# Two-block transformer layer on one core: sliding-window attention units of eight heads instead of four, one small sum on GpSimd, other pacing of stream transposes and first norm

## The chip, the core and the metric

One NeuronCore of one Trainium2 chip runs the whole program. The engines are TensorE (PE in the profile; PEld is its weight load), VectorE (DVE), ScalarE (ACT), GpSimd (POOL) and SyncE (SP, which issues the DMAs here). The metric is the device time of one execution in microseconds, median of three runs.

## The reference

Input is `x` of 512 tokens by 1024 features. Two blocks follow each other. Everything is float32.

The first block normalises `x`, projects it eight ways, does a four-head differential attention and a short gated convolution, projects back, adds, and gates in a per-layer embedding. The second block has a gated MLP (layer A) and then layer B, sliding-window attention with sinks and ALiBi, which the change touches:

```python
q, z = jnp.split(h @ w_in, 2, axis=-1)          # b_w_in_2: 1024 -> 2 x 1024
q = q * (HEAD_DIM ** -0.5)                       # 16 heads of 64, 4 key/value heads
...
logits = jnp.einsum('btkgd,bskd->bkgts', qb, kb).astype(jnp.float32) + alibi
logits = jnp.where(valid, logits, -jnp.inf)      # blocks of 128 queries, 256 keys (first: 128)
m = jnp.maximum(jnp.max(logits, axis=-1), sink)
p = jnp.exp(logits - m[..., None])
denom = jnp.sum(p, axis=-1) + jnp.exp(sink - m)
o = jnp.einsum('bkgts,bskd->btkgd', p.astype(vb.dtype), vb).astype(jnp.float32)
o = o / denom.transpose(0, 3, 1, 2)[..., None]
...
y = out * jax.nn.silu(z)
return y @ w_out                                 # b_w_out_2: 1024 -> 1024
```

The result is normalised, scaled and added to the residual stream `h`.

## The kernel before, in words

**Numbers as pairs.** A float32 operand of a large matmul is split into a high and a low part (`...h`, `...l`): ScalarE copies the high part, VectorE subtracts it from the source for the low part (`gsplit`, `wsplit`). Each product is then three matmuls (`mm3`: high-high, high-low, low-high). Weights come by DMA (`raw`), are split into `whi` and `wlo` in halves of 512 columns, and are used once.

**Who sets the order.** The program is unrolled in Python, and a small planner (`Flow`) decides in which order instructions are written. The main stream is the large matmuls. Everything else is generators; each `yield` says what the next piece waits for: tiles, a condition, or a number of nanoseconds of the planner's PE time. After every three matmuls `F.tick()` lets those continue whose time has come, and what they issue is written at that place. So the planner's costs and the PACE numbers fix, at build time, the order on every engine; on the chip each engine works strictly in that order. When the main stream needs an operand that no generator has delivered yet, `F.until` lets waiting generators go on first.

**The start.** The first projection (`w_in`) runs while `first_stat` forms the sum of squares of `x`: eight squares on ScalarE, seven sums `sq` on VectorE. `norm(st, D, "n1")` then writes the column sums (`st`, four small matmuls), the power on GpSimd and the broadcast (`bc`), and the evictions of the first projection wait for the result.

**Layer B.** The main stream is 16 column blocks of `b_w_in` (24 matmuls each): blocks 0 to 7 give the queries (`QB`), blocks 8 to 15 the gate (`bz`, then `bzt`, `bzs`, in `SZB`). Then comes `b_w_out`, in two halves of two token blocks; in each half the features `k` = 0 to 7 follow each other, so that the attention output `YB[k, t]` is needed for `k` = 4 only after 24 matmuls. `swa_master` spawns an attention unit every PACE_B: for a head group `pr` (0, 1), a block `b` of 128 queries (0 to 3) and a half `s`, four heads. A unit writes, with waits between: eight score matmuls (`bsc`), four additions with running maximum on VectorE (`be`, `bmx`), `bneg` and a sum `bdn` with the sink (VectorE, four elements wide), four exponentials with row sums (ScalarE), the denominator and its reciprocal `brd` (VectorE), the normalisation of two heads on GpSimd and two on ScalarE, per key block four transposes (`btr`) and their split (`bph`, `bpl`), the product with the values (`bpv`), and the joining into `y` (`pc` on ScalarE, `y` on VectorE). The second of the two units of a (`pr`, `b`) then multiplies `y` by the gate in four pieces and splits it into `ybh` and `ybl`, which `b_w_out` reads.

**The end.** `h_tokens` transposes the residual stream back to tokens (`ht`, eight groups of four transposes, PACE_H apart), and `ev_last` scales, adds it and stores.

Of the kernel before, what the change touches and what calls it, by code (L numbers as in the profile page):

```python
# [43 lines left out]
KLATE = 3  # L44
BANKS = 7

PACE_A, PACE_B, PACE_LN, PACE_H = 4500, 3500, 8000, 7000
WARM = 10


# [103 lines left out]
def block(ctx: ExitStack, tc: tile.TileContext, xT, pT, w_in, w_out, w_ple, w_gate, a_w_in, a_w_out,  # L154
# [27 lines left out]
    def pst(name):  # L182
        live[0] += name in COUNTED
        return psum.tile([P, T], F32, tag="ps", name=nm(name))

    def pfree(n=1):
        live[0] -= n

    def banks(n):
        return lambda: live[0] + n <= BANKS  # L190

    def sm(name, n):
        return small.tile([P, n], F32, tag=f"s{n}", name=nm(name), bufs=40 if n == NT else 6)

    def size(a):
        return math.prod(a.shape[1:])
# [4 lines left out]
    def act(o, a, func, bias=0.0, scale=1.0, accum_out=None, after=0.0):  # L201
        nc.scalar.activation(o, a, func, bias=bias, scale=scale, accum_out=accum_out)  # L202
        ex = is_ap(bias, scale, accum_out)
        F.op("act", 80 + 0.84 * size(o) + 93 * len(ex), [o] + is_ap(accum_out), [a] + is_ap(bias, scale), after)

    def stt(o, a, sc, b, op0, op1):
        nc.vector.scalar_tensor_tensor(o, a, sc, b, op0, op1)
        F.op("dve", 70 + 1.04 * size(o) + 65 * len(is_ap(sc)), [o], [a, b] + is_ap(sc))

    def tt(o, a, b, op, after=0.0):  # L210
        nc.vector.tensor_tensor(o, a, b, op)  # L211
        F.op("dve", 70 + 1.04 * size(o), [o], [a, b], after)
# [40 lines left out]
    def transpose(o, a):  # L253
        nc.tensor.transpose(o, a, ident)
        F.op("pe", 114, [o], [a])
# [121 lines left out]
    def gsplit(src, d, key, name, gain=None, dst=None):  # L377
        hi, lo = dst or rt2(name)
        if gain is None:
            act(hi, src, AF.Copy)  # L380
        else:
            act(hi, src, AF.Copy, scale=gain)
        yield [hi]
        if gain is None:
            tt(lo, src, hi.bitcast(F32), ALU.subtract)
        else:
            stt(lo, src, gain, hi.bitcast(F32), ALU.mult, ALU.subtract)
        if d is not None:
            d[key] = (hi, lo)
# [62 lines left out]
    def norm(stat, d, name, n=1024, eps=EPS, copy=True, half=None):  # L452
        key = name if half is None else (name, half)
        yield lambda: all(stat.n[h] == stat.total for h in ((0, 1) if half is None else (half,)))
        yield stat.acc if half is None else [stat.acc[half]]
        r = cols(stat.acc, n, eps, half)
        d[name + "c" if half is None else (name + "c", half)] = r
        yield [r]
        if name in WIDE:
            os = []  # L460
            yield from bcast_wide(r, os)
            o = os[0]
        else:
# [179 lines left out]
    def scores(o, q, k):  # L643
        mm(o, q, k[0], True, False)
        mm(o, q, k[1], False, True)
# [468 lines left out]
    sinkp = const.tile([P, 16], F32, name="sinkp")  # L1114
    tt(sinkp, row[:, R_SINK:R_SINK + 16], cst[:, H_ISL:H_ISL + 16], ALU.mult)

    PO = {}

    def swa_unit(pr, b, s):
        nb = 1 if b == 0 else 2  # L1120
        kw = nb * P
        ksl = slice((b + 1) * P - kw, (b + 1) * P)
        bq = slice(b * P, (b + 1) * P)
        h0 = 8 * pr + 4 * s
        mx = sm("bmx", 4)
        sums = sm("bsum", 4)
        yield banks(2)
        os = [pst("bsc"), pst("bsc")]
        oo = [os[i // 2][:, (i % 2) * 256:(i % 2) * 256 + kw] for i in range(4)]
        for i in range(4):  # L1130
            scores(oo[i], QB[4 * pr + i][s][:, bq], [a[:, ksl] for a in KS[pr][s]])
        yield os
        es = [rt("be"), rt("be")]
        ev = [es[i // 2][:, (i % 2) * 256:(i % 2) * 256 + kw] for i in range(4)]
        for i in range(4):
            addmax(ev[i], oo[i], tbB[:, 256 - kw:], sinkp[:, h0 + i:h0 + i + 1], mx[:, i:i + 1])
        pfree(2)
        neg = sm("bneg", 4)
        tt(neg, mx, cst[:, H_NSL + h0:H_NSL + h0 + 4], ALU.mult)
        for i in range(4):  # L1140
            act(ev[i], ev[i], AF.Exp, bias=neg[:, i:i + 1], scale=SLOPE_B[h0 + i], accum_out=sums[:, i:i + 1])
        dn = sm("bdn", 4)
        tt(dn, neg, row[:, R_SINK + h0:R_SINK + h0 + 4], ALU.add)
        act(dn, dn, AF.Exp)
        yield [dn]
        tt(dn, dn, sums, ALU.add)
        rd = sm("brd", 4)
        recip(rd, dn)
        for i in range(4):
            if i < 2:  # L1150
                nc.gpsimd.tensor_scalar(ev[i], ev[i], rd[:, i:i + 1], None, ALU.mult)
                F.op("pool", 450 + 2.37 * size(ev[i]), [ev[i]], [ev[i], rd])
        yield [rd]
        for i in range(2, 4):
            act(ev[i], ev[i], AF.Copy, scale=rd[:, i:i + 1])
        yield es
        hd = 2 * pr + s
        pts = []
        for kb in range(nb):
            yield banks(1)  # L1160
            o = pst("btr")
            for i in range(4):
                transpose(o[:, i * P:(i + 1) * P], ev[i][:, kb * P:(kb + 1) * P])
            pts.append({})
            yield from gsplit(o, pts[-1], 0, "bp")
            pfree()
        yield [a for p in pts for a in p[0]]
        yield lambda: all(b - nb + 1 + kb in VZ for kb in range(nb))
        yield banks(1)
        o = pst("bpv")  # L1170
        for kb in range(nb):
            v = VZ[b - nb + 1 + kb][:, hd * P:(hd + 1) * P]
            for j in range(2):
                mm(o, v, pts[kb][0][j], kb == j == 0, kb == nb - 1 and j == 1)

        own, other = (LO, HI) if s == 0 else (HI, LO)
        yield [o]
        c = rt("pc")
        act(c[own], o[other], AF.Copy)
        yield [c]  # L1180
        if (pr, b) not in PO:
            PO[pr, b] = [rt("y4"), 0]
        y = PO[pr, b][0]
        tt(y[own], o[own], c[own], ALU.add)
        pfree()
        PO[pr, b][1] += 1
        if PO[pr, b][1] == 2:
            yield lambda: all(4 * pr + i in SZB for i in range(4))
            yield [y, SZB[4 * pr + 3]]
            for i in range(4):  # L1190
                yi = y[:, i * P:(i + 1) * P]
                stt(yi, yi, 0.5, SZB[4 * pr + i][:, bq], ALU.mult, ALU.mult)
            got = {}
            yield from gsplit(y, got, 0, "yb")
            for i in range(4):
                YB[4 * pr + i, b] = [a[:, i * P:(i + 1) * P] for a in got[0]]

    def swa_master():
        for pr, b in ORDER_B:
            yield lambda: pr in KS and all(4 * pr + i in QB for i in range(4))  # L1200
            yield [q for i in range(4) for q in QB[4 * pr + i]] + [k for ks in KS[pr] for k in ks]
            for s in range(2):
                F.spawn(swa_unit(pr, b, s))
                yield PACE_B

    HT = {}

# [166 lines left out]
```

## Time and profile before

| | us |
|---|---|
| median of 3 runs (lowest, highest) | 894.44 (894.09, 894.47) |
| profiled execution, its own time | 895.67 |
| its span, first to last instruction | 893.9 |
| PE busy in it | 881.7 |
| DVE busy | 640.9 |
| ACT busy | 444.2 |
| POOL busy | 72.4 |
| granted clock of PE, mean (share of 2.4 GHz) | 0.999 |

The span is that of the profiled execution, which took 1.23 us longer than the median. A matmul of 512 columns is shown with some 0.39 us, but the next starts about 0.23 us after it: they overlap, and the distance of two starts is the price in a row of them. DVE and ACT instructions overlap by some 0.08 us in the same way.

### The profile page before, as it was taken

The numbers are of one execution on the slowest core, as the hardware profiler recorded it, in microseconds if no ns is written. First come the engines' busy times: TensorE is split into PE (matmuls) and PEld (weight loads), VectorE is DVE, ScalarE is ACT, GpSimd is POOL, SyncE is SP. The second block draws the span as 40 slices with busy tenths as digits, with TensorE's granted clock in tenths as the row PEclk, the third lists the DMA queues.
The fourth block names the chain that finished last, engine by engine and source line by source line (L and its number), as shares of the span: only waits on it lengthen the run. The fifth ranks groups of instructions, "written<-read, shape, count | busy, mean of one in ns | idle before, by whom it ended". The sixth has DMA issues, their size and how long they took to land.

```text
span 893.9 us, 12071 instructions
## 1 busy us (share of the span) xinstructions
PE 881.7 (99%) x4348; PEld 743.6 (83%) x4348; DVE 640.9 (72%) x1380; ACT 444.2 (50%) x954; POOL 72.4 (8%) x77
## 2 busy tenths in 40 slices
PE   8999999999999999999999999999999999999997
PEld 7888888888888888888888888888899988888786
DVE  6899989653558883338897766683347876999974
ACT  7456554322556544335443333322444646998764
POOL 0100113000000001001000000000000001433000
PEclk9999999999999999999999999999999999999999
DMA  7231221225423243232232222314232258211362
GB/s 262 95 119 48 68 99 48 95 94 189 142 71 117 72 134 107 98 105 79 74 112 86 83 95 95 95 51 138 94 121 69 71 145 216 65 48 48 118 198 108
DMA packets 30444, 93.21 MB, mean 104 GB/s; under 512 B 3888, under 2 KB 4272, under 8 KB 30384
## 3 DMA queue, kind: packets, MB, share of 16 engines
q1 hardware_dynamic: 30384, 92.44, 31.8%
q8 instruction: 34, 0.56, 0.3%
q14 instruction: 26, 0.21, 0.1%
HBM read 85.60 MB, written 2.10 MB: 98 GB/s over the span
## 4 chain that ended last, share of the span: by engine, by line
PE 89%; DVE 6%; DMA 1%; ACT 1%; issue 1%; SPq 1%; DVEq 0%; ACTq 0%
PE a_w_in L244 29%; PE w_in L244 18%; PE a_w_out L244 10%; PE b_w_in L244 6%; PE w_gate L244 5%; PE w_out L244 5%; PE b_w_out L244 5%; PE kv L244 3%; PE sp L244 2%; PE e L244 1%; PE sc L244 1%; DVE be L227 1%; PE bsc L244 1%; DVE bpl L211 1%; PE pv L244 1%
## 5 line engine op out<-in xcount | busy, mean ns | idle before, releaser
L211 DVE TENSOR_TENSOR wlo<-raw,whi 128x512 fp32r<-128x512 f32 x280 | 190.5, 708 | 97.4 <-ACT whi L202 96.9
L202 ACT ACTIVATE whi<-raw 128x512 fp32r<-128x512 f32 x280 | 165.5, 623 | 128.5 <-PE a_w_in L244 39.4
L244 PE MATMUL a_w_in<-h2h,whi 128*128 128x512 f32 x256 | 99.8, 390 | 0.0
L244 PE MATMUL a_w_in<-h2l,whi 128*128 128x512 f32 x256 | 99.7, 390 | 0.0
L244 PE MATMUL a_w_in<-h2h,wlo 128*128 128x512 f32 x256 | 99.6, 389 | 0.0
L244 PE MATMUL w_in<-h1h,whi 128*128 128x512 f32 x224 | 88.5, 397 | 0.9 <-ACT h1h L202 0.9
L244 PE MATMUL w_in<-h1h,wlo 128*128 128x512 f32 x224 | 87.0, 391 | 0.0
L244 PE MATMUL w_in<-h1l,whi 128*128 128x512 f32 x224 | 86.9, 390 | 0.0
L215 POOL TENSOR_TENSOR rstd<-var,mhalf 128x4 f32<-128x4 f32 (+2 forms) x15 | 14.1, 939 | 593.5 <-DVE var L222 536.7
L244 PEld LDWEIGHTS a_w_in<-h2h,wlo 128*128 128x128 f32 x256 | 48.1, 188 | 9.9
L244 PEld LDWEIGHTS a_w_in<-h2h,whi 128*128 128x128 f32 x256 | 48.1, 188 | 9.7
L244 PEld LDWEIGHTS a_w_in<-h2l,whi 128*128 128x128 f32 x256 | 48.1, 188 | 9.6
L211 DVE TENSOR_TENSOR sq<-sq,sq 128x512 f32<-128x512 f32 (+1 forms) x44 | 29.3, 666 | 36.3 <-ACT sq L202 34.4
L244 PE MATMUL b_w_in<-hbh,whi 128*128 128x512 f32 x128 | 52.0, 406 | 0.0
L244 PE MATMUL b_w_in<-hbh,wlo 128*128 128x512 f32 x128 | 50.1, 391 | 0.0
L244 PE MATMUL b_w_in<-hbl,whi 128*128 128x512 f32 x128 | 50.1, 391 | 0.0
L244 PE MATMUL a_w_in<-whi,h2h 128*128 128x512 f32 x128 | 50.0, 391 | 0.0
L244 PE MATMUL a_w_in<-whi,h2l 128*128 128x512 f32 x128 | 49.8, 389 | 0.0
L244 PE MATMUL a_w_in<-wlo,h2h 128*128 128x512 f32 x128 | 49.8, 389 | 0.0
L244 PEld LDWEIGHTS w_in<-h1h,whi 128*128 128x128 f32 x224 | 42.0, 188 | 9.2 <-ACT h1h L202 1.1
L244 PEld LDWEIGHTS w_in<-h1h,wlo 128*128 128x128 f32 x224 | 42.0, 188 | 9.0
L244 PEld LDWEIGHTS w_in<-h1l,whi 128*128 128x128 f32 x224 | 42.1, 188 | 8.1
(269 smaller groups left out, 2029.8 us busy)
## 6 DMA issues: line engine op xcount, KB each, us to landing
raw<-in_a_w_in SPq DMA_DIRECT2D x48, 512.0 KB, 3.2
raw<-in_w_in SPq DMA_DIRECT2D x29, 512.0 KB, 3.2
raw<-in_a_w_out SPq DMA_DIRECT2D x16, 512.0 KB, 3.2
raw<-in_b_w_in SPq DMA_DIRECT2D x16, 512.0 KB, 3.5
raw<-in_b_w_out SPq DMA_DIRECT2D x16, 512.0 KB, 3.7
raw<-in_w_out SPq DMA_DIRECT2D x8, 512.0 KB, 3.3
raw<-in_w_gate SPq DMA_DIRECT2D x8, 512.0 KB, 3.3
x<-in_xT SPq DMA_DIRECT2D x8, 256.0 KB, 5.7
```

What stands on the lines that cost most here:

```text
L202: nc.scalar.activation(o, a, func, bias=bias, scale=scale, accum_out=accum_out)
L211: nc.vector.tensor_tensor(o, a, b, op)
L215: nc.gpsimd.tensor_tensor(o, a, b, op)
L227: nc.vector.tensor_tensor_reduce(o, a, b, 1.0, s0, ALU.add, ALU.max, mx)
L244: nc.tensor.matmul(o, a, b, start=start, stop=stop)
```

## The change

One unit now takes the eight heads of a (`pr`, `b`). It makes two rounds of scores and additions (`s` = 0, 1), then one `bneg`, one sum with the sink (eight wide, now on GpSimd), eight exponentials, one denominator and one reciprocal, four normalisations on GpSimd and four on ScalarE, and then per `s` transposes, product and joining; the gate follows. Units start 7000 ns apart (a pair of the old ones took 2 x 3500), the `ht` groups 4000 instead of 7000 ns apart, and `norm` of `n1` waits 1500 ns of the planner's time before its `st` matmuls are written. The buffers of the small tiles follow the new widths.

```diff
-PACE_A, PACE_B, PACE_LN, PACE_H = 4500, 3500, 8000, 7000
+PACE_A, PACE_B, PACE_LN, PACE_H = 4500, 7000, 8000, 4000
...
+        if name == "n1":
+            yield 1500
         r = cols(stat.acc, n, eps, half)
...
-    def swa_unit(pr, b, s):
+    def swa_unit(pr, b):
...
+        mx = sm("bmx", 8)
+        sums = sm("bsum", 8)
+        es = []
+        for s in range(2):
+            yield banks(2)
+            os = [pst("bsc"), pst("bsc")]
...
+            for i in range(4):
+                h = 4 * s + i
+                addmax(es[h // 2][:, (i % 2) * 256:(i % 2) * 256 + kw], oo[i], tbB[:, 256 - kw:],
+                       sinkp[:, h0 + h:h0 + h + 1], mx[:, h:h + 1])
+            pfree(2)
...
+        neg = sm("bneg", 8)
+        tt(neg, mx, cst[:, H_NSL + h0:H_NSL + h0 + 8], ALU.mult)
+        dn = sm("bdn", 8)
+        nc.gpsimd.tensor_tensor(dn, neg, row[:, R_SINK + h0:R_SINK + h0 + 8], ALU.add)
+        F.op("pool", 300, [dn], [neg])
+        for h in range(8):
+            act(ev[h], ev[h], AF.Exp, bias=neg[:, h:h + 1], scale=SLOPE_B[h0 + h], accum_out=sums[:, h:h + 1])
...
+        for h in range(8):
+            if h % 4 < 2:
+                nc.gpsimd.tensor_scalar(ev[h], ev[h], rd[:, h:h + 1], None, ALU.mult)
...
-            for s in range(2):
-                F.spawn(swa_unit(pr, b, s))
-                yield PACE_B
+            F.spawn(swa_unit(pr, b))
+            yield PACE_B
```

Three places of the order. The first is PE at the start of the program, where the four `st` matmuls (column sums of the squares, `sq`) stand among the matmuls of the first projection:

```order
 L244 MATMUL w_in_192<-h1l_176,whi_166 128x512
 L244 MATMUL w_in_192<-h1h_175,wlo_167 128x512
-L244 MATMUL st_299<-ones,sq_209 128x1 x4
 L244 MATMUL w_in_193<-h1h_175,whi_166 128x512
 L244 MATMUL w_in_193<-h1l_176,whi_166 128x512
...
 L244 MATMUL w_in_191<-h1l_181,whi_237 128x512
 L244 MATMUL w_in_191<-h1h_180,wlo_238 128x512
+L244 MATMUL st_314<-ones,sq_209 128x1 x4
```

The sums moved behind nine more matmuls, of which the last is the first to read `wlo_238`.

The second place is VectorE in the order before, from the eviction of the last `b_w_in` block (`bz`, it needs that block's last matmul) to the low part of the output of (`pr`, `b`) = (1, 1), `ybl_8193`; (1, 0) is `ybl_8166`:

```order
L211 TENSOR_TENSOR bz_8070<-b_w_in_7963,n6rb_6574 128x512
L211 TENSOR_TENSOR bpl_8010<-btr_8004,bph_8009 128x512
L211 TENSOR_TENSOR bpl_8029<-btr_8023,bph_8028 128x512
...
L207 SCALAR_TENSOR_TENSOR y_1706_8110<-y_1706_8110,bzs_8122 128x128
L211 TENSOR_TENSOR ybl_8166<-y_1654_7918,ybh_8165 128x512
L211 TENSOR_TENSOR y_1729_8207<-bpv_8149,pc_8172 64x512
L211 TENSOR_TENSOR wlo_8155<-raw_8035,whi_8154 128x512
L211 TENSOR_TENSOR ybl_8193<-y_1706_8110,ybh_8192 128x512
```

These are 28 instructions, both ends counted: 20 of 512 columns and 8 pieces of the gate of 128.

The same stretch of VectorE in the changed kernel, again from the eviction of the last `b_w_in` block to the output of (1, 1), here `ybl_8150` (`y_1544`); (1, 0) is `ybl_8011`:

```order
L211 TENSOR_TENSOR bz_7934<-b_w_in_7840,n6rb_6574 128x512
L211 TENSOR_TENSOR wlo_7763<-raw_7574,whi_7762 128x512
L211 TENSOR_TENSOR wlo_7842<-raw_7691,whi_7841 128x512
L211 TENSOR_TENSOR ybl_7885<-y_1430_7080,ybh_7884 128x512
L211 TENSOR_TENSOR bpl_7894<-btr_7888,bph_7893 128x512
...
L211 TENSOR_TENSOR ybl_8011<-y_1512_7428,ybh_8010 128x512
...
L211 TENSOR_TENSOR bpl_8141<-btr_8135,bph_8140 128x512
L211 TENSOR_TENSOR y_1577_7689<-bpv_8129,pc_8143 64x512
L211 TENSOR_TENSOR ybl_8150<-y_1544_7552,ybh_8149 128x512
```

They are now 49: 33 of 512 columns (9 `wlo`, 9 `bpl`, 8 `y` from `bpv`, 5 `ybl`, `bz`, `bzs`) and 16 pieces of the gate, those of (1, 0), (0, 2), (0, 3) and (1, 1). The outputs of (0, 1), (1, 0), (0, 2) and (0, 3) are in it too; before, of these only (1, 0) was.

The third place is PE in the changed kernel, around the matmul that reads `ybl_8150`, the 30th of `b_w_out`:

```order
L244 MATMUL b_w_out_7942<-whi_7944,ybl_8011 128x512
L254 MATMUL ht_8081<-ident,y_5675 128x128
...
L244 MATMUL bpv_8161<-bph_8140,vz_6602 128x512
L244 MATMUL bpv_8161<-bpl_8141,vz_6602 128x512
L244 MATMUL b_w_out_7943<-whi_7944,ybh_8149 128x512
L244 MATMUL b_w_out_7943<-wlo_7945,ybh_8149 128x512
L244 MATMUL b_w_out_7943<-whi_7944,ybl_8150 128x512
```

From the last matmul of `b_w_in` to the last row here, PE has 29 other matmuls of `b_w_out`, 28 `bpv`, seven groups of four `btr` transposes and two groups of four `ht`; before, up to the matmul that reads `ybl_8193`, it had 29 and 20, six groups of `btr` and none of `ht`. All eight `ht` groups now stand ahead of the last `b_w_out` matmul; before, the last three (12 transposes) stood behind it.

## Rows read from the trace of the kernel before

**Rows 1.** The page, part 1: busy time of each engine over the span.
```profile
PE 881.7 (99%) x4348; PEld 743.6 (83%) x4348; DVE 640.9 (72%) x1380; ACT 444.2 (50%) x954; POOL 72.4 (8%) x77
```

**Rows 2.** Waits of PE over the whole span: total, times, longest (us).
```profile
PE b_w_out L244 <- DVE ybl L211: 1.8, 1, 1.8
PE st L244 <- DVE sq L211: 1.0, 1, 1.0
PE bsc L244 <- DMA qh<-ql: 0.7, 1, 0.7
PE btr L254 <- DVE bpl L211: 0.3, 1, 0.3
PE rs L244 <- ACT gv L202: 0.2, 1, 0.2
```

**Rows 3.** Busy time by stretch: us, then PE, PEld, DVE, ACT, POOL.
```profile
795.00:847.00 52.00, 49.75 (x261) 40.40 (x260) 51.07 (x143) 45.15 (x115) 12.65 (x13) 1.00 0.22 73
```

**Rows 4.** Timeline, 17 to 31 us, PE, then DVE: start, duration, instruction.
```profile
20.99 0.39 PE L244 MATMUL w_in<-h1h,wlo 128*128 128x512 f32 x1
22.38 1.05 PE L244 MATMUL st<-ones,sq 128*128 128x1 f32 x8 [1.00 <-DVE sq L211]
...
22.24 1.89 DVE L211 TENSOR_TENSOR wlo<-raw,whi 128x512 fp32r<-128x512 f32 x3
```

**Rows 5.** The chain that ended last, 700 to 894 us: start, us, what.
```profile
836.03 0.44 PE btr L254 x4
...
844.88 1.83 PE bpv L244 x8
...
848.51 6.85 PE b_w_out L244 x30
```

**Rows 6.** Timeline, 826 to 849 us, PE.
```profile
830.00 0.40 PE L244 MATMUL b_w_in<-hbh,wlo 128*128 128x512 f32 x1
...
844.38 0.50 PE L244 MATMUL b_w_out<-whi,ybl 128*128 128x512 f32 x1 [1.76 <-DVE ybl L211]
...
847.00 0.39 PE L244 MATMUL b_w_out<-whi,ybl 128*128 128x512 f32 x1
```

**Rows 7.** Timeline, 826 to 848 us, DVE.
```profile
831.47 0.68 DVE L211 TENSOR_TENSOR bpl<-btr,bph 128x512 fp32r<-128x512 f32 x1
832.07 0.68 DVE L211 TENSOR_TENSOR bz<-b_w_in,n6rb 128x512 f32<-128x512 f32 x1
...
842.83 0.89 DVE L207 SCALAR_TENSOR_TENSOR y<-y,bzs 128x128 f32<-128x128 f32 x4
843.64 0.69 DVE L211 TENSOR_TENSOR ybl<-y,ybh 128x512 fp32r<-128x512 f32 x1
...
845.44 0.68 DVE L211 TENSOR_TENSOR ybl<-y,ybh 128x512 fp32r<-128x512 f32 x1
```

**Rows 8.** Instruction groups, 740 to 894 us, DVE: busy, mean ns, idle before.
```profile
L231 DVE RECIPROCAL brd<-bdn 128x4 f32<-128x4 f32 x16 | 2.9, 178 | 0.5
L211 DVE TENSOR_TENSOR bneg<-bmx,cst 128x4 f32<-128x4 f32 x16 | 2.6, 162 | 0.6
```

**Rows 9.** Instruction groups, 700 to 894 us, POOL.
```profile
L1151 POOL TENSOR_SCALAR be<-be,brd 128x256 f32<-128x256 f32 x24 | 24.3, 1026 | 41.3 <-ACT be L202 25.6 <-ACT whi L202 6.1 <-DVE brd L231 5.9
```

**Rows 10.** Line 1151's instructions: duration ns min/median/max, first and last start.
```profile
L1151 POOL TENSOR_SCALAR be<-be,brd x32: 599/926/1722, 749.2 to 828.2; 128x256 f32<-128x256 f32 x24, 128x128 f32<-128x128 f32 x8
```

**Rows 11.** Instruction groups, 700 to 894 us, ACT.
```profile
L202 ACT ACTIVATE be<-be,bneg 128x256 f32<-128x256 f32 (+1 forms) x64 | 30.0, 472 | 7.9 <-DVE bneg L211 7.7
```

**Rows 12.** Timeline, 876 to 894 us, all engines.
```profile
886.15 0.39 PE L244 MATMUL b_w_out<-wk,ybl 128*128 128x512 f32 x1
886.38 1.47 PE L254 MATMUL ht<-ident,y 128*128 128x128 f32 x12
...
887.54 0.55 POOL L215 TENSOR_TENSOR rstd<-var,mhalf 128x1 f32<-128x1 f32 x1 [2.18 <-DVE var L207]
887.97 2.73 DVE L207 SCALAR_TENSOR_TENSOR y<-y,rstd,ht 128x512 f32<-128x512 f32 x4
```

More of the change, by code (lines that the diff above doesn't have):

```diff
@@ L192, in sm @@
     def sm(name, n):
-        return small.tile([P, n], F32, tag=f"s{n}", name=nm(name), bufs=40 if n == NT else 6)
+        return small.tile([P, n], F32, tag=f"s{n}", name=nm(name), bufs=16 if n == NT else 25 if n == 8 else 6)
     def size(a):
@@ L1115, in block @@
     tt(sinkp, row[:, R_SINK:R_SINK + 16], cst[:, H_ISL:H_ISL + 16], ALU.mult)
-    PO = {}
-    def swa_unit(pr, b, s):
+    def swa_unit(pr, b):
         nb = 1 if b == 0 else 2
@@ L1123, in swa_unit @@
         bq = slice(b * P, (b + 1) * P)
[L1124 to L1143, printed above, removed]
+        h0 = 8 * pr
+        mx = sm("bmx", 8)
[4 more added lines that the diff above has]
+            os = [pst("bsc"), pst("bsc")]
+            oo = [os[i // 2][:, (i % 2) * 256:(i % 2) * 256 + kw] for i in range(4)]
+            for i in range(4):
+                scores(oo[i], QB[4 * pr + i][s][:, bq], [a[:, ksl] for a in KS[pr][s]])
+            yield os
+            es += [rt("be"), rt("be")]
+            for i in range(4):
+                h = 4 * s + i
+                addmax(es[h // 2][:, (i % 2) * 256:(i % 2) * 256 + kw], oo[i], tbB[:, 256 - kw:],
+                       sinkp[:, h0 + h:h0 + h + 1], mx[:, h:h + 1])
+            pfree(2)
+        ev = [es[h // 2][:, (h % 2) * 256:(h % 2) * 256 + kw] for h in range(8)]
+        neg = sm("bneg", 8)
[5 more added lines that the diff above has]
+            act(ev[h], ev[h], AF.Exp, bias=neg[:, h:h + 1], scale=SLOPE_B[h0 + h], accum_out=sums[:, h:h + 1])
         act(dn, dn, AF.Exp)
@@ L1146, in swa_unit @@
         tt(dn, dn, sums, ALU.add)
-        rd = sm("brd", 4)
+        rd = sm("brd", 8)
         recip(rd, dn)
-        for i in range(4):
[L1150 to L1196, printed above, removed]
+        for h in range(8):
+            if h % 4 < 2:
+                nc.gpsimd.tensor_scalar(ev[h], ev[h], rd[:, h:h + 1], None, ALU.mult)
+                F.op("pool", 450 + 2.37 * size(ev[h]), [ev[h]], [ev[h], rd])
@@ new lines, in swa_unit @@
+        yield [rd]
+        for h in range(8):
+            if h % 4 >= 2:
+                act(ev[h], ev[h], AF.Copy, scale=rd[:, h:h + 1])
+        y = rt("y4")
+        for s in range(2):
+            yield es[2 * s:2 * s + 2]
+            pts = []
+            for kb in range(nb):
+                yield banks(1)
+                o = pst("btr")
+                for i in range(4):
+                    transpose(o[:, i * P:(i + 1) * P], ev[4 * s + i][:, kb * P:(kb + 1) * P])
+                pts.append({})
+                yield from gsplit(o, pts[-1], 0, "bp")
+                pfree()
+            yield [a for p in pts for a in p[0]]
+            yield lambda: all(b - nb + 1 + kb in VZ for kb in range(nb))
+            yield banks(1)
+            o = pst("bpv")
+            hd = 2 * pr + s
+            for kb in range(nb):
+                v = VZ[b - nb + 1 + kb][:, hd * P:(hd + 1) * P]
+                for j in range(2):
+                    mm(o, v, pts[kb][0][j], kb == j == 0, kb == nb - 1 and j == 1)
+            own, other = (LO, HI) if s == 0 else (HI, LO)
+            yield [o]
+            c = rt("pc")
+            act(c[own], o[other], AF.Copy)
+            yield [c]
+            tt(y[own], o[own], c[own], ALU.add)
+            pfree()
@@ L1198, in swa_master @@
+        yield lambda: all(4 * pr + i in SZB for i in range(4))
+        yield [y, SZB[4 * pr + 3]]
+        for i in range(4):
+            yi = y[:, i * P:(i + 1) * P]
+            stt(yi, yi, 0.5, SZB[4 * pr + i][:, bq], ALU.mult, ALU.mult)
+        got = {}
+        yield from gsplit(y, got, 0, "yb")
+        for i in range(4):
+            YB[4 * pr + i, b] = [a[:, i * P:(i + 1) * P] for a in got[0]]
     def swa_master():
```

## The prediction, made before the changed kernel ran

> **What bounds the kernel now.** I read the busy times first: PE is busy for 881.7 of 893.9 us [rows 1]. A stream that dense can only gain where PE stands still, so the next view is the list of PE's waits [rows 2]. The reader is to see how short it is: 1.8 us before a `b_w_out` matmul that waits for the low part of the attention output, 1.0 us before the `st` sums, 0.7 us before the first scores (a DMA that moves query rows), 0.3 and 0.2 us elsewhere. None of those shown lies in the first block's attention, where units are interleaved in the same way. Since the change leaves the count of PE's instructions as it is, the question is only what becomes of these waits and whether new ones come.
>
> Third, what limits PE where it waits in layer B. From 795 to 847 us DVE is busy for 51.07 of 52 us and ACT for 45.15 [rows 3]: DVE has no room there, and whatever PE needs from it comes when its queue has come that far. The timelines of both engines [rows 6, 7] show the mechanism. PE starts the last matmul of `b_w_in` at 830.00. DVE evicts that block (`bz`) at 832.07, so it is 1.8 us behind; it ends the output of (1, 0) shortly after 844.3, where PE waits for it, and that of (1, 1) at 846.1, before PE reads it at 847.00.
>
> **Prices.** A matmul of 512 columns in a row costs 0.23 us (6.85 us for 30, 1.83 us for 8), a group of four transposes 0.44 us [rows 5]. DVE starts a 512-column instruction 0.60 us after the last (831.47, 832.07) and takes 0.81 us for four pieces of the gate (842.83 to 843.64) [rows 7].
>
> **The start.** PE's last matmul ahead of the sums starts at 20.99, so the next could start at 21.22; the `st` matmul starts at 22.38 [rows 4]. That is 1.16 us lost. With the sums nine matmuls later PE does 9 x 0.23 = 2.1 us of work first. The ninth, at 21.22 + 8 x 0.23 = 23.05, reads the first half of `wlo_238`. DVE starts three `wlo` at 22.24, of about 0.68 us each, so the first ends at 22.92 [rows 4]: just in time. The squares are summed by 22.3, so the sums no longer wait. The bounds are 0 (DVE late by a microsecond) and -1.16; I take **-1.1 us**, since both times are read off the trace. The broadcast of the norm falls six matmuls (1.4 us) further back in the order, which the 1.1 us nearly pay back; the evictions behind it shift by 0.3 us. As PE did not wait there before [rows 2], I cost that at 0; without that cover it is 0.3 us, and at worst the gain is lost again.
>
> **Fewer small VectorE instructions.** Each unit pair had two `bneg`, two sums with the sink, two of the denominator and two reciprocals; now it has one, none, one and one. That is 8 x 5 = 40 fewer: 32 of about 0.16 us and 8 of 0.18 us [rows 8], 6.6 us of busy time. Eight elements in place of four I price the same, as both are almost all fixed cost; the bounds are 0 and twice the row, and the total stays negative. But all of them, before and after, stand ahead of the eviction of the last `b_w_in` block, and this eviction can't begin before PE has ended that block. Work saved ahead of it makes DVE wait there. What it can give back is the 1.8 us by which DVE is behind now. So this term is not added; it is inside the next one.
>
> **The end of layer B.** The order sets what DVE must do between that eviction and the output of (1, 1), and what PE has to do meanwhile.
>
> - Before: PE has 29 matmuls of `b_w_out`, 20 `bpv` and six groups of transposes, 49 x 0.23 + 6 x 0.44 = 13.9 us. The trace has 847.00 - 830.23 = 16.8 us [rows 6], so 2.9 us are lost (the two waits, and transposes drawn out between them).
> - After: PE has 29 + 28 matmuls and nine groups, 57 x 0.23 + 9 x 0.44 = 17.0 us. DVE has 33 instructions of 512 columns and 16 pieces: 33 x 0.60 + 16 x 0.20 = 23.1 us. It can't start before the block's last matmul has ended (0.2 us after its place, as 0.40 us is its length), and 0.1 us pass at the other end. So PE gets `ybl_8150` after 23.4 us and has lost 6.4 us on the way.
>
> The difference is **+3.5 us**. Of the 17.0 us, 0.9 us are two `ht` groups that formerly came later; that is not a loss, and I counted lost time alone. The reason is not a slower DVE. The larger units end later and closer together: four outputs ahead of (1, 1) fall into the stretch, and those of (0, 2) and (0, 3), which nothing needs before the second half of `b_w_out`, stand ahead of the one that PE waits for. Bounds: 3.1 if the drawn-out transposes of before recur in the 17.0 us (they would then hide under the wait), 5.5 if DVE's own waits (2% in rows 3, 0.4 us) and a wait of PE for a free PSUM bank ahead of the block's end (0.3 us in rows 2, perhaps 1 us with five `btr` groups in a short space) come on top.
>
> **GpSimd.** Its added sum I bound by nothing and 0.55 us, the one-column power [rows 12]; it is needed after eight exponentials, 8 x 0.47 = 3.8 us of ACT [rows 11], and costs 0 under them. Without them it is 0.55 us on each of eight units, on ACT and not on PE. Four normalisations in a row take 4 x 1.03 = 4.1 us instead of two runs of 2.05 [rows 9]. For the last unit PE's order has 58 matmuls and seven groups between its scores and its first transposes, 16 us, which covers the 3.8 us, half of the run, and what lies between: 0.
>
> **The tail.** All `ht` groups now precede the last matmul. It comes 12 x 0.11 = 1.3 us later for that. Behind it, before, four final `y` ran from 887.97 to 890.70, 4.55 us after that matmul's start at 886.15 [rows 12], two of them only because their `ht` copy was late. After, the last two follow the power, which ended at 887.54 + 0.55 = 888.09, 1.94 us after that start, and take 2 x 0.68 us: 3.3 us. That is 1.25 us less, in sum **+0.1 us**.
>
> **Sum.** -1.1 + 3.5 + 0.1 = +2.5 us: 896.4 for the span of 893.9, 898.2 for the profiled execution of 895.67. Its 1.23 us above the median are its own, so I add the change to the median: **896.9 us**, 0.28% slower. A measurement of this kernel tells about 0.2% (1.8 us) from no change.
>
> **The rivals.**
>
> *VectorE's relief reaches PE: faster.* DVE is full from 795 us on, and 6.6 us of busy time go away there. If the stretch at the end were limited by DVE's backlog alone, the 2.9 us lost there would vanish too: -1.1 - 2.9 + 0.1 = -3.9, 890.5 us; with half of it 892. For it speaks rows 3. Against it: the backlog at the eviction is 1.8 us and no more [rows 6, 7], and the stretch behind it grows from 28 to 49 instructions. It decides where the 23.1 us become less than 20; that needs six of the 33 instructions moved out, and the order is fixed.
>
> *Break-even.* PE's lost time grows by only 1 to 2 us, because before also lost time that I can't place, or because the start gives its whole 1.16 us and the 0.2 us of smaller waits go: -1.3 + 1.5 + 0.1 = +0.3, 894.7; up to 896.2. That the moved sums and transposes change nothing that can be measured belongs here too (894.4).
>
> *More waits on top.* The start's gain is used up by DVE in the first attention stage (+1.1: 898.0), or PE waits for PSUM banks while DVE stands before an eviction (+1 us: 897.9); both: 899.
>
> *GpSimd held up.* One and the same form of normalisation takes between 0.60 and 1.72 us with a median of 0.93 [rows 10], so something holds it up. If each of a run of four took 1.72 us, the run would take 6.9 us and a unit's second transposes come 2.8 us later; if that reached PE once, 899.7. Against it stands the cover of 16 us for the last unit.
> The Trainium skill, "SBUF — State Buffer", section "Who interferes with whom", says that a VectorE instruction with two SBUF inputs and a GpSimd instruction that reads SBUF block each other for a whole instruction. That speaks against giving GpSimd more to do beside a full VectorE, and the spread of rows 10 is in keeping with it. By this rule alone each of the four could wait for one VectorE instruction.
>
> **Chances.** Forecast (896.0 to 897.8) 0.52; more waits 0.15; GpSimd 0.03; break-even 0.23; faster 0.07. The range takes in break-even for the most part and the added waits up to one and a half of them: **894.8 to 898.8**. Slower by over 0.2% means above 896.23, which is 0.48 of the forecast's 0.52 and both cases above it: 0.66. Faster (below 892.65): 0.07. The rest, 0.27, is within 0.2%.
>
> **What would show it.** The wait before `st` is gone and PE starts the second block of `w_in` a microsecond earlier. DVE stands still for some microseconds ahead of the last two `bz`, and then not once up to `ybl` of (1, 1), 23 us later. PE's waits for DVE (`b_w_out` for `ybl`, `bpv` for `bpl`) add up to 5 to 7 us in place of 2.1, within some 17 us of matmuls after the last `b_w_in`. No `ht` stands behind the last `b_w_out`. The forecast is wrong if PE's waits there stay under 4 us, which means that DVE went through the stretch faster than 0.60 us each or PE came to it later; or if new waits stand ahead of 795 us.

## The result, and the profile after

The changed kernel takes 899.97 us (median of 4 runs, 899.58 to 901.39) where the kernel before takes 894.46 (4 runs): ratio 1.0057, 95% interval 1.0045 to 1.0068. Timed again, it took 901.06 against 894.79, 1.0071 (1.0057 to 1.0086). It is 5 to 6 us slower; 2.5 us were forecast. Its profiled execution took 899.96 us, with a span of 898.2, which is 4.3 us over the span of before.

Busy time over the span in the changed kernel, then those of PE's waits there that are new or longer than in [rows 2]:

```profile
PE 883.1 (98%) x4348; PEld 743.9 (83%) x4348; DVE 635.0 (71%) x1340; ACT 442.3 (49%) x946; POOL 74.6 (8%) x85
```
```profile
PE b_w_out L244 <- DVE ybl L211: 3.0, 2, 2.5
PE bpv L244 <- DVE bpl L211: 2.6, 3, 1.1
...
PE tr L254 <- DVE s L207: 0.4, 1, 0.4
PE b_w_out L244 <- DVE bpl L211: 0.3, 1, 0.3
```

PE's busy time is the same within 1.4 us. The wait ahead of `st` is gone and so is the one wait of `btr`; in their place PE waits 3.0 us for `ybl`, 2.6 and 0.3 for `bpl`, and 0.4 us for a new neighbour of the start (`tr`). [rows 2] leaves out two waits at the very start, 1.1 us of `warm` and 0.9 of the first `w_in`; here they are 1.1 and 0.5.

The end of layer B, which answers to [rows 6]: PE's timeline in the changed kernel from the last matmul of `b_w_in` to the one that reads `ybl` of (1, 1).

```profile
826.88 0.40 PE L244 MATMUL b_w_in<-hbh,wlo 128*128 128x512 f32 x1
...
840.94 0.50 PE L244 MATMUL b_w_out<-whi,ybl 128*128 128x512 f32 x1 [2.48 <-DVE ybl L211]
...
846.35 0.50 PE L244 MATMUL bpv<-bpl,vz 128*128 128x512 f32 x1 [1.06 <-DVE bpl L211]
...
851.85 0.50 PE L244 MATMUL b_w_out<-whi,ybl 128*128 128x512 f32 x1 [0.49 <-DVE ybl L211]
```

From 827.11 (the place after the last `b_w_in`) to 851.85 are 24.74 us, in which PE has 57 matmuls and nine groups of transposes: 57 x 0.23 + 9 x 0.44 = 17.07. It loses 7.7 us; before, 2.9.

VectorE in the same stretch, which answers to [rows 7]: some of its 49 instructions.

```profile
827.32 0.69 DVE L211 TENSOR_TENSOR bz<-b_w_in,n6rb 128x512 f32<-128x512 f32 x1 [0.54 <-PE b_w_in L244]
...
833.68 0.69 DVE L211 TENSOR_TENSOR y<-bpv,pc 64x512 f32<-64x512 f32 x1
834.41 0.69 DVE L211 TENSOR_TENSOR bpl<-btr,bph 128x512 fp32r<-128x512 f32 x1
835.13 0.69 DVE L211 TENSOR_TENSOR y<-bpv,pc 64x512 f32<-64x512 f32 x1
...
837.99 0.67 DVE L211 TENSOR_TENSOR y<-bpv,pc 64x512 f32<-64x512 f32 x1
...
840.81 0.68 DVE L211 TENSOR_TENSOR wlo<-raw,whi 128x512 fp32r<-128x512 f32 x1
841.41 0.68 DVE L211 TENSOR_TENSOR bpl<-btr,bph 128x512 fp32r<-128x512 f32 x1
...
851.10 0.69 DVE L211 TENSOR_TENSOR ybl<-y,ybh 128x512 fp32r<-128x512 f32 x1
```

It stands idle for 0.54 us ahead of `bz`, then never waits, and ends `ybl` at 851.79: 24.5 us for what the prediction priced at 23.1. Most starts lie 0.60 us apart (840.81, 841.41), but 833.68, 834.41 and 835.13 some 0.72: the `y` at 833.68 and 835.13 are second halves, which fill the upper 64 partitions of their tile; the one at 837.99 is a first half.

Where VectorE stood still before that, its waits from 745 to 853 us in the kernel before and then in the changed one (total, times, longest):

```profile
DVE be L227 <- PE bsc L244: 2.3, 4, 1.0
...
DVE bdn L211 <- ACT bdn L202: 1.3, 2, 1.0
...
DVE bz L211 <- PE b_w_in L244: 0.2, 1, 0.2
```
```profile
DVE be L227 <- PE bsc L244: 7.4, 6, 2.9
DVE bdn L211 <- ACT bdn L202: 4.4, 3, 2.1
DVE bz L211 <- PE b_w_in L244: 2.3, 2, 1.8
```

For these three its idle time is 3.8 us before and 14.1 after. From 795 to 830 us it is busy for 30.38 us in the changed kernel (first line, third figure), where before it was busy for 34.23:

```profile
795.00:830.00 35.00, 34.86 (x188) 28.98 (x186) 30.38 (x80) 34.03 (x88) 12.75 (x14) 1.00 0.19 64
```
```profile
795.00:830.00 35.00, 34.87 (x188) 28.72 (x186) 34.23 (x110) 32.13 (x91) 12.65 (x13) 1.00 0.14 46
```

The 49 instructions behind the last `bz`, 28 before, are fixed by the order. The idle time is the other side of it: VectorE stands still ahead of `bz`, while work that it could have done is written behind it.

The tail, which answers to [rows 12]:

```profile
891.57 0.39 PE L244 MATMUL b_w_out<-wk,ybl 128*128 128x512 f32 x1
...
893.59 1.41 DVE L207 SCALAR_TENSOR_TENSOR y<-y,rstd,ht 128x512 f32<-128x512 f32 x2
```

From the last `b_w_out` matmul to the end of the span are 6.6 us, before 7.75 (893.9 - 886.15); the 12 transposes that moved ahead cost 1.3: +0.2 us.

### The profile page after: what moved, and what is told of

Same layout as the page of the kernel before. It is cut to its first block, busy times and chain, and to the rows that moved or that the text cites. A ratio compares the mean times of both kernels' runs of the same rounds, so it can differ in the third digit from the quotient of the medians.

```text
span 898.2 us, 12006 instructions
## 1 busy us (share of the span) xinstructions
PE 883.1 (98%) x4348; PEld 743.9 (83%) x4348; DVE 635.0 (71%) x1340; ACT 442.3 (49%) x946; POOL 74.6 (8%) x85
## 4 chain that ended last, share of the span: by engine, by line
PE 90%; DVE 6%; issue 1%; DMA 1%; ACT 1%; SPq 0%; DVEq 0%; ACTq 0%
PE a_w_in L244 28%; PE w_in L244 17%; PE a_w_out L244 10%; PE b_w_in L244 9%; PE w_gate L244 5%; PE w_out L244 5%; PE b_w_out L244 4%; PE kv L244 3%; PE sp L244 2%; PE bsc L244 2%; DVE wlo L211 1%; PE e L244 1%; PE btr L254 1%; PE bpv L244 1%; PE sc L244 1%
```

## The experiments

Each group was timed in turn with the kernel before on one chip, 5 to 11 executions of each variant. The groups ran on different chips, so it is the ratios to the kernel before that compare.

**One part at a time.** The kernel before as it is, and with the later sums alone:

```diff
         yield stat.acc if half is None else [stat.acc[half]]
+        if name == "n1":
+            yield 1500
```

> The kernel before, unchanged, for a second profile. Two theories on why the changed kernel is 5.5 us above the median of before, where its profiled execution is only 4.3 us above that of before. Start theory: the profiled execution of before lost some 1.2 us at the start (1.0 us ahead of `st`, 0.9 us ahead of the first `w_in`) that most executions don't lose; then this profile shows a span near 892.7, under 0.3 us ahead of `st`, and the sums moved back gain nothing. Spread theory: the wait of about 1.0 us ahead of `st` stands here again, and the span differs by something else. In both the median is 894.5.

> Before with one part of the change, the 1500 ns ahead of the first norm's sums. The prediction's price is -1.1 us: 893.4. By the start theory (most executions don't lose that microsecond) 894.4, no change. If the broadcast, which comes 1.4 us later in the order, makes DVE late: up to 895.

Measured: before_again 894.77 us (ratio 1.0001, 0.9992 to 1.0009); start_alone 895.18 (1.0002, 0.9993 to 1.0011). PE's wait for the squares in the second profile of before, and then one form of the `kv` matmuls, which come behind the whole first block, in that profile and in that of start_alone (durations in ns, first and last start):

```profile
PE st L244 <- DVE sq L211: 0.6, 1, 0.6
```
```profile
L244 PE MATMUL kv<-resh,wk x64: 279/283/363, 681.7 to 704.7; 128*128 128x256 f32 x64
```
```profile
L244 PE MATMUL kv<-resh,wk x64: 279/283/363, 681.5 to 704.6; 128*128 128x256 f32 x64
```

The wait ahead of `st` was 1.0 us in the first profile and is 0.6 here; in that of units_alone, below, which has the sums in their old place, no such wait is listed. The edit removes it, and 0.3 us ahead of `tr` come in its stead. The first `kv` matmul starts at 681.7 without the edit (682.1 in the first profile) and at 681.5 with it, and at 681.4 in units_alone without it. So most of the microsecond belonged to the one execution that I had read: the edit gives nothing that can be measured, and a gain of the full 1.1 us lies outside the interval, which allows 0.6. The span of before is 892.9 here and 893.9 in the first profile, so that the changed kernel is 5.3 us over the one and 4.3 over the other.

The two edits that aren't the units, and the units alone (with their spacing and the sum on GpSimd):

```diff
# old_units: the kernel before with
+            yield 1500
+PACE_A, PACE_B, PACE_LN, PACE_H = 4500, 3500, 8000, 4000
# units_alone: the changed kernel without them
-            yield 1500
+PACE_A, PACE_B, PACE_LN, PACE_H = 4500, 7000, 8000, 7000
```

> The change without its eight-head units: four-head units, 3500 apart, all sums on VectorE; the later first sums and the closer `ht` groups stay. If the units alone make the change slower, this is no slower than before: 893.5 by the prediction's terms for start and tail (-1.1 and +0.1), 894.6 by the start theory. If the `ht` groups or the start cost time themselves, above 895.5.

> Before with the eight-head units (their spacing of 7000 and the sum on GpSimd with them); sums of the first norm and `ht` groups as before. VectorE's queue theory: the whole loss is in the stretch from the last `bz` to the output of (1, 1), some 24.5 us of VectorE work against 16.6 us of matmuls: PE's waits for `ybl` and `bpl` there are 5 to 7 us, and the time 899 to 901. If the start or the `ht` groups have part in the loss: under 898.

Measured: old_units 895.62 us (1.0006, 0.9997 to 1.0015); units_alone 901.91 (1.0074, 1.0062 to 1.0087). The units make the whole loss, 7.0 us by themselves, which is over the 899 to 901 that was expected. The profile of units_alone showed something that the changed kernel's first profile doesn't: the granted clock (the figure ahead of the last two) by stretch of a microsecond, and PE's matmuls behind the two pauses.

```profile
838.00:839.00 1.00, 0.00 (x0) 0.00 (x0) 1.00 (x7) 0.26 (x1) 0.00 (x0) 1.00 0.00 0
...
842.00:843.00 1.00, 1.00 (x4) 0.81 (x3) 1.00 (x3) 0.94 (x2) 0.00 (x0) 0.50 0.86 352
844.00:845.00 1.00, 1.00 (x11) 0.91 (x10) 1.00 (x3) 0.00 (x0) 0.00 (x0) 1.00 0.00 0
...
854.00:855.00 1.00, 1.00 (x4) 0.80 (x3) 0.30 (x3) 0.88 (x2) 0.00 (x0) 0.50 0.00 0
...
857.00:858.00 1.00, 1.00 (x6) 0.81 (x5) 1.00 (x2) 0.38 (x1) 0.00 (x0) 1.00 0.00 0
```
```profile
840.12 0.80 PE L244 MATMUL b_w_out<-whi,ybl 128*128 128x512 f32 x1 [2.49 <-DVE ybl L211]
...
851.09 0.79 PE L244 MATMUL b_w_out<-whi,ybh 128*128 128x512 f32 x1 [1.81 <-ACT ybh L202]
...
854.24 0.63 PE L244 MATMUL b_w_out<-whi,ybl 128*128 128x512 f32 x1
854.66 0.63 PE L244 MATMUL b_w_out<-whi,ybh 128*128 128x512 f32 x1
...
893.42 0.39 PE L244 MATMUL b_w_out<-wk,ybl 128*128 128x512 f32 x1
```

PE paused for 2.49 and for 1.81 us; behind each pause the clock stands at 0.50, which is 1.2 of 2.4 GHz, and the next matmul of a row starts 0.42 us after the last (854.24 to 854.66) instead of 0.23. The second pause names ScalarE's `ybh`, but ScalarE stood 2.27 us waiting for VectorE's `y` ahead of it: it is the same queue, and with this wait PE's add up to the 5 us that were expected there.

**What GpSimd has to do with it, and what the instructions in the stretch cost.** The sum back on VectorE at the same place; the gate and split of (0, 2) and (0, 3) held back; their whole second half held back:

```diff
# sum_on_vector
-        nc.gpsimd.tensor_tensor(dn, neg, row[:, R_SINK + h0:R_SINK + h0 + 8], ALU.add)
+        nc.vector.tensor_tensor(dn, neg, row[:, R_SINK + h0:R_SINK + h0 + 8], ALU.add)
# gate_late, ahead of the gate; half_late, ahead of the transposes
+        if pr == 0 and b >= 2:
+            yield lambda: (4, 1) in YB
```

> The changed kernel itself, unchanged, as the baseline for the next three and for a second profile. Queue theory: PE's waits for `ybl` and `bpl` in the last stretch of layer B add up to 5 to 7 us again, the stretch from the last `b_w_in` matmul to the output of (1, 1) takes about 24.9 us, median 899.5 to 900.5. Clock theory, in addition: where PE pauses for about 2.5 us its granted clock falls to 0.50 for some microseconds in some executions (it did in the profile of the units alone, not in the first profile of the changed kernel); then runs with a mean clock under 0.996 are 1 to 2 us slower than those with 0.998.

> The changed kernel with the sum of sink and maximum on VectorE again, at the same place of the program (the order of all other instructions stays). GpSimd theory (it holds up units or VectorE): faster by more than 0.5 us. Queue theory: no change within 0.9 us of the changed kernel, since the eight added instructions of about 0.16 us lie ahead of the last `bz`, where VectorE waits for PE; 900.

> The changed kernel with the gate and split of (0, 2) and (0, 3) held back until the output of (1, 1) is written. This takes 2 outputs and 4 pieces of the gate out of the stretch up to (1, 1) (31 wide instructions and 12 pieces in place of 33 and 16, some 2.0 us), and 8 pieces in place of none are out of the part up to (1, 0). Queue theory: PE's waits there fall by about 2.0 us, time 897.5 to 898.5. Rival (the units, the GpSimd or the clock cost the time, not those instructions): within 0.9 us of the changed kernel.

> The changed kernel with the whole second half of (0, 2) and (0, 3) (transposes, products, gate, split) held back until the output of (1, 1) is written. The stretch up to (1, 1) then has 24 wide instructions and 8 pieces (16.0 us, with the drawn-out ones some 17) against 45 matmuls and eight groups of transposes (13.9 us): PE loses some 3.4 us there in place of 7.7. Queue theory: 4.3 us faster than the changed kernel, 895 to 896.5, if the work held back isn't late for the second half of `b_w_out`. Rival: less than half of that.

Measured: changed_again 901.06 us; sum_on_vector 901.99 (1.0077, 1.0065 to 1.0089); gate_late 897.87 (1.0035, 1.0023 to 1.0047); half_late 896.32 (1.0019, 1.0011 to 1.0028). The sum on GpSimd costs nothing that can be measured. PE's timeline at the end of the stretch in changed_again, gate_late and half_late:

```profile
826.35 0.40 PE L244 MATMUL b_w_in<-hbh,wlo 128*128 128x512 f32 x1
...
851.31 0.50 PE L244 MATMUL b_w_out<-whi,ybl 128*128 128x512 f32 x1 [0.48 <-DVE ybl L211]
```
```profile
826.52 0.40 PE L244 MATMUL b_w_in<-hbh,wlo 128*128 128x512 f32 x1
...
849.44 0.50 PE L244 MATMUL b_w_out<-whi,ybl 128*128 128x512 f32 x1 [0.87 <-DVE ybl L211]
```
```profile
821.87 0.39 PE L244 MATMUL b_w_in<-hbh,wlo 128*128 128x512 f32 x1
...
839.58 0.80 PE L244 MATMUL b_w_out<-whi,ybl 128*128 128x512 f32 x1 [0.33 <-DVE ybl L211]
```

Between the two rows lie 24.96, 22.92 and 17.71 us: gate_late takes 2.04 us out of the stretch for the 2.0 that were priced, and 2.1 to 3.2 us out of the time. half_late has 13.9 us of matmuls in it and loses 3.6 where 3.4 were expected. Its longest wait, 1.6 us, is for ScalarE's `ybh`, which itself waits for VectorE's `y`. So what PE loses there goes with the instructions in VectorE's queue between the two places.

**The clock.** Matmuls on old data in the two pauses of units_alone; the first attempt put them into the second pass over `b_w_out` too, where there is no pause:

```diff
+        y = need(YB, (k, t))
+        if (k, t) in FILL and not FILLED.get((k, t)):   # FILL = {(4, 0): 10, (4, 1): 7}
...
+            for _ in range(FILL[k, t]):
+                nc.tensor.matmul(junk, YB[0, 0][0], YBF[0, 0], start=True, stop=True)
```

> The units alone (901.9 us, its profile at a granted clock of 0.50 from 839.8 to 843 and from 849.9 to 856.4 us, after pauses of PE of 2.5 and 1.8 us), with 10 and 7 matmuls of 512 columns on old data put into the two pauses of PE (ahead of the first `b_w_out` matmuls of k = 4, token blocks 0 and 1); their results are read by nothing, and the order of everything else stays. Clock theory (the pauses cost the clock, and the clock costs 1.5 to 2.5 us behind the second one): the clock stays at 1.00 there and the time is 899 to 900.3. Rival (the lower clock hides under VectorE's queue, or comes without the pauses): 901 or more.

> The units alone (901.9 us) with 10 and 7 matmuls of 512 columns on old data in the two pauses of PE, this time in the first pass over `b_w_out` only (before they stood in the second as well, where PE had no pause: 17 x 0.23 = 3.9 us of added work, by which its 903.6 would be 899.7). Clock theory: the clock stays at 1.00 behind the pauses and the time is 899 to 900.3, though PE has more to do. Rival (the lower clock costs nothing, or the filling lengthens the pauses): 901 or more.

Measured: units_filled 903.64 us (1.0091, 1.0078 to 1.0104); units_filled_once 900.07 (1.0059, 1.0046 to 1.0073). In the profile of the second the clock (the figure ahead of the last two) stays up. The second fence has its first matmul on the output of (1, 1) and its last of `b_w_out`:

```profile
844.00:850.00 6.00, 3.84 (x14) 2.30 (x14) 5.88 (x13) 2.55 (x5) 0.00 (x0) 1.00 0.61 178
850.00:857.00 7.00, 6.77 (x31) 5.02 (x30) 6.00 (x17) 5.02 (x10) 0.00 (x0) 1.00 0.00 0
```
```profile
850.96 0.50 PE L244 MATMUL b_w_out<-whi,ybh 128*128 128x512 f32 x1 [0.21 <-ACT ybh L202]
...
890.95 0.39 PE L244 MATMUL b_w_out<-wk,ybl 128*128 128x512 f32 x1
```

The first had 17 x 0.23 = 3.9 us of matmuls too many; the second took 3.6 us less than it. Against units_alone the filled kernel is 1.8 us faster by its median, though PE does more; but the intervals overlap, and two of its five executions took 901.7 and 902.0. So the medians alone do not show the gain, and the profiles place it. From the last `b_w_in` matmul to the first on the output of (1, 1) are 25.03 us in both: behind the first pause the lower clock costs nothing, since PE waits for VectorE there anyway. From there to the last matmul of `b_w_out` (851.09 to 893.42, and 850.96 to 890.95) are 42.3 and 40.0 us: behind the second pause it costs 2.3.

Other executions speak for the same. Of the ten of the changed kernel seven had a mean clock of 0.997 or more and a median of 899.96 us (one took 902.25), three had 0.993 or 0.994 and took 901.39, 901.77 and 903.75. Of the eleven of order_before_2, below, four with 0.999 or more took 895.2 to 895.9 us, and seven with 0.996 to 0.998 took 897.1 to 899.7. In units_alone the mean clock does not sort the five times (900.8 at 0.994, 901.8 at 0.997).

**Other orders and spacings.** The four outputs that the first half of `b_w_out` reads first, for the changed kernel and for the one before, and a third order; the eight-head units 4000 apart; (1, 2) and (1, 3) held back in the kernel before:

```diff
# order_changed, order_before
+ORDER_B = ((0, 0), (0, 1), (1, 0), (1, 1), (0, 2), (0, 3), (1, 2), (1, 3))
# order_before_2
+ORDER_B = ((0, 0), (0, 1), (0, 2), (1, 0), (1, 1), (0, 3), (1, 2), (1, 3))
# spacing_4000
+PACE_A, PACE_B, PACE_LN, PACE_H = 4500, 4000, 8000, 4000
# late_before, ahead of the transposes
+        if pr == 1 and b >= 2:
+            yield lambda: (4, 1) in YB
```

> The changed kernel with the units in another order: (0,0), (0,1), (1,0), (1,1), (0,2), (0,3), (1,2), (1,3), so that the four outputs that the first half of `b_w_out` reads come first. The stretch from the last `bz` to the output of (1, 1) then has 35 wide instructions and 12 pieces on VectorE (23.6 us, some 25 with the drawn-out ones) against 65 matmuls and 17 groups of transposes on PE (22.4 us): PE loses about 2.9 us in place of 7.7. Queue theory: 895, between 893.5 and 896.5, 5 us less than the changed kernel with the same eight-head units. Rival (eight-head units or GpSimd cost the time by themselves): 898 or more.

> The kernel before with the same other order of its units. The stretch then has 15 wide instructions, 8 pieces and 4 tiny ones on VectorE (11.0 us and a backlog of about 2) against 49 matmuls and 13 groups (17.0 us): VectorE is ahead and PE's waits for `ybl` and `bpl` vanish. Queue theory: 2 to 2.9 us faster than before, 892 to 893. Rival: PE's pauses move to other places (the outputs of (0, 2) and (0, 3), now later): no faster than before.

> The kernel before with a third order: (0,0), (0,1), (0,2), (1,0), (1,1), (0,3), (1,2), (1,3). VectorE has 11 wide instructions and 12 pieces (9.0 us) between the last `bz` and the output of (1, 1), PE 41 matmuls and no transposes (9.4 us). Queue theory: PE loses what VectorE is behind at that `bz`, 0.3 to 2 us, and the time lies between the two others: 892.5 to 894.5. Rival: no faster than before.

> The changed kernel with the eight-head units 4000 apart in place of 7000. VectorE has 19 wide instructions and 12 pieces (13.8 us, some 14.7 with the drawn-out ones) from the last `bz` to the output of (1, 1), PE 41 matmuls and three groups of transposes (10.8 us). Queue theory (units that start sooner use VectorE's idle time ahead of that stretch): PE loses about 4.2 us there in place of 7.7, time 896 to 898, a microsecond more if VectorE is behind at that `bz`. Rival (eight-head units cost the time wherever they stand): 899.5 or more.

> The kernel before with the second half of the units of (1, 2) and (1, 3) (transposes, products, gate, split) held back until the output of (1, 1) is written. VectorE then has 13 wide instructions and 8 pieces (9.4 us) in the stretch, PE 37 matmuls (8.5 us). Queue theory: PE loses 1.2 to 2 us in place of 2.9, and the time is 893 to 894.2. Rival (VectorE is behind at the last `bz`, or the work held back makes PE wait later): 894.5 or more, no faster than before.

Measured: order_changed 901.29 us (1.0073, 1.0055 to 1.0091); order_before 895.68 (1.0011, 1.0001 to 1.0020); order_before_2 897.23 (1.0017, 1.0005 to 1.0030); spacing_4000 902.82 (1.0085, 1.0070 to 1.0099); late_before 897.69 (1.0026, 1.0015 to 1.0036). None of the five came out as the queue theory had it; each landed on its rival's side. Waits of VectorE in order_changed, of PE in order_before, and of VectorE in spacing_4000:

```profile
DVE bdn L211 <- ACT bdn L202: 9.4, 4, 3.0
```
```profile
PE btr L254 <- DVE y L211: 1.7, 1, 1.7
PE bpv L244 <- ACT ht L202: 1.5, 1, 1.5
...
PE bpv L244 <- DVE bpl L211: 0.6, 1, 0.6
```
```profile
DVE bz L211 <- PE b_w_in L244: 11.3, 5, 3.9
```

The count of the stretch held for the place that it was made for: in order_before PE no longer waits for `ybl`. But it waits 3.8 us for other things on VectorE and ScalarE, where before it waited 2.1 us for `ybl` and `bpl` [rows 2]. In order_changed VectorE stands for 9.4 us at the denominators, behind ScalarE's exponentials, and PE for 2.9 us ahead of one `btr`; with units 4000 apart it stands for 11.3 us at `bz` evictions that are written into its queue long before PE has the block, and what queues behind them is late again. Its PE waits 4.7 us for the two parts of an output of layer B and then loses the clock (0.53 from 850 to 854 us). I had counted what lies behind the last `bz`, not when VectorE reaches it. late_before moved the wait as well (1.6 us for `ybh` of (1, 1)), and order_before_2 made the one for `ybl` longer (2.8 us). Both lost the clock in their profiles, so part of their loss may be the clock's.

**Which property of the units.** Four-head units started two at a time; and an eight-head unit with a softmax for each half:

```diff
# paired_units
                 F.spawn(swa_unit(pr, b, s))
-                yield PACE_B
+            yield 2 * PACE_B
# split_softmax, for each s: bneg, bdn, four exponentials, sum, reciprocal
+        for s in range(2):
+            neg = sm("bneg", 4)
...
+            recip(rd, dn)
```

> The kernel before with its four-head units started two at a time, every 7000 (as the eight-head units are), instead of one every 3500. VectorE has 15 wide instructions and 8 pieces (10.6 us) from the last `bz` to the output of (1, 1), PE 45 matmuls and two groups of transposes (11.2 us). Unit theory (the eight-head unit's serial chain pushes VectorE's work behind the last `bz`; starting together doesn't): PE loses at most what VectorE is behind at that `bz`, some 2 us as before; 894 to 896. Bunching theory: 898 or more.

> The changed kernel's eight-head unit, in which each half of four heads has its own negated maximum, sum with the sink (on GpSimd), four exponentials, denominator and reciprocal; scores of both halves first, and transposes, products and gate behind both, as in the changed kernel. VectorE has 34 wide instructions and 16 pieces (23.6 us) against 16.6 us of PE's work in the stretch, as the changed kernel has. Unit theory (what counts is the serial unit and where its second half lies): 899 to 902, as the changed kernel. Softmax theory (VectorE's wait behind eight exponentials is the loss): 897 or less.

Measured: paired_units 897.97 us (1.0040, 1.0026 to 1.0054); split_softmax 901.19 (1.0065, 1.0052 to 1.0077). Splitting the softmax gives nothing back: in its profile VectorE waits less for the scores and denominators, but 7.6 us at `bz`, where the changed kernel waits 2.3. Starting heads in eights costs about 3 us by itself, but in another place: PE's waits in paired_units are in the middle of layer B, for banks that VectorE has not emptied, and at the end there is 0.5 us left for `ybl`.

```profile
PE bpv L244 <- DVE bmx L227: 1.1, 1, 1.1
...
PE bpv L244 <- DVE bz L211: 0.9, 1, 0.9
PE bsc L244 <- DVE bpl L211: 0.8, 1, 0.8
...
PE b_w_out L244 <- DVE ybl L211: 0.5, 1, 0.5
```

This fits neither theory: not the 894 to 896 of the one, and not the other's place.

## Why the prediction was wrong, point by point

**The start (-1.1 us): wrong.** The failed step is "both times are read off the trace": they were, but of one execution. The wait is 1.0, 0.6, 0.3 and 0.2 us in four of the nine profiles with that order of the start and is not listed in the other five, and the edit alone changes the time by nothing that can be measured. I wrote that the 1.23 us by which the first profile exceeded its median were "its own" and still booked the wait as a gain. Against the second profile of before, the first is 0.4 us later at the first `kv`, and another 0.5 us is the wait for the query rows ahead of `bsc` (0.7 against 0.2).

**Fewer small instructions (nothing by itself): right.** VectorE's busy time fell by 5.9 us (640.9 to 635.0) and its idle time ahead of the last `bz` grew by more than that (3.8 to 14.1).

**The end of layer B (+3.5): right mechanism, too small.** PE lost 7.7 us for 2.9 before, +4.8, and its waits for VectorE add up to the 5 to 7 us that were named as the sign. The mis-sized factor is 0.60 us for each wide instruction: 24.5 us in place of 23.1. Ten of the distances were about 0.72, on both sides of the five `y` instructions that write the second half (partitions 64 to 127) of a tile; the stretch before had one such `y`. That is 1.2 of the 1.4 us by which the stretch ran longer. The Trainium skill, "VectorE: DVE Perf Modes", section "Two Vector instructions with no wait between them", says that an instruction whose input or output starts in another group of 32 partitions than the last one in the same memory is held until every earlier one has finished. The trace agrees: 0.72 us is the whole 0.69 us of an instruction and a little, and `y` of the first halves (837.99, 846.82) start 0.60 us after the one before. An eleventh distance of 0.71 us (836.67 to 837.38) is at no such `y` and stays unexplained. The prediction's own sums are also a tenth off twice: 33 x 0.60 + 16 x 0.20 is 23.0 and 57 x 0.23 + 9 x 0.44 is 17.1, by which its term would be +3.4.

**GpSimd (nothing): right.** The sum on VectorE is no faster. The rival's 899.7 us lies next to the measured 899.97 by luck: in the changed kernel a run of four normalisations takes 2.6 to 4.4 us, not 6.9, and no engine is listed as waiting for one there. The rival also misread [rows 10], which mixes two widths: the 0.60 us belongs to 128 columns, and with 256 none took under 0.92.

**The tail (+0.1): right**, +0.2.

**What was missing.** The granted clock. I priced PE's pauses by their length; in some executions the clock falls at the end of the stretch, and the matmuls behind it then take some 2 us more. The changed kernel pauses for 2.5 us where before paused for 1.8. And the base: the changed time was added to the median, but a term of it was taken from what made the profiled execution longer than the median.

With the measured terms the sum is 0 + 4.8 + 0.2 = 5.0 us, and about 2 us more in the executions that lose the clock: 5 to 7 us over 894.5, where 5.5 and 6.3 were measured. Some 0.5 us of the 5.5 has no place in this sum.

Shown are that the units make the loss and VectorE's idle time ahead of the stretch (units_alone), and that instructions in the stretch cost PE their length (gate_late, half_late). What stays open: which property of the eight-head unit sets the idle time. Sharing one softmax is not it, and starting in eights costs about 3 us, but elsewhere. The count of the stretch did not predict the time of any other order or spacing. No version beat the kernel before.

## What to carry over

Where two engines are both full, count the work that a slower one must do between two places that the other pins, but count it at both ends: work taken away ahead of the first place turns into idle time, and work moved behind it into a stall. Before a wait of one microsecond is booked as a gain, look whether a second execution has it. A pause of the matrix engine can cost more than its length, if its clock falls and nothing behind it hides the slower matmuls.

## What the runs showed of the hardware

In units_alone PE's clock fell to 0.50 (1.2 of 2.4 GHz) during pauses of PE of 2.49 us and, after some busy microseconds, of 1.81 us with another 0.70 shortly before; it stood there until about 843 and 856.5. The same pause of 2.48 us left it at 1.00 in the first profile of the changed kernel. It fell also in the profiles of half_late, order_before_2, spacing_4000, late_before and split_softmax, in or shortly behind waits of PE of 1.4 to 2.8 us. VectorE's distance of 0.60 us between 512-column instructions is 0.72 on both sides of one that writes the upper 64 partitions, with others that don't around it.
